# Adding up four of a pair's seven products in one PSUM bank of a Strassen-Winograd matmul

## The chip, the core and the metric

The kernel runs on one core of one Trainium2 chip. The metric is the device time of one execution in microseconds (us). Three runs of the kernel before took 1344.66, 1345.26 and 1346.1 us; their median is 1345.26 us.

## What is computed

One layer of a decoder trunk on x (1 x 1024 x 1024, float32), cut to what matters here:

```python
xn = rmsnorm(x, norm_mix_w)
proj = xn @ w_in                        # 34 blocks of 128 columns
merged = sigmoid(g_da) * (diff_attention(...) @ w_br_da) + sigmoid(g_sw) * (sliding_window(...) @ w_br_sw)
x = x + merged @ w_mix_out
u = rmsnorm(x, norm_ffn_w) @ w_up       # 44 blocks: 22 gate, 22 value
c = causal_conv3(u) + conv_b
x = x + (silu(c_gate) * c_val) @ w_down
return rmsnorm(x, norm_final_w)
```

## The kernel before

All activations are held transposed: channels on the 128 partitions, the 1024 tokens along the free axis. Each float32 operand is split into a high part (a cast to fp32r by ScalarE, tag `wh`, `sh`) and a low part (the rest, by a VectorE subtraction, tag `wl`, `sl`), and each product of blocks is three matmuls: high x high, high x low, low x high.

The stages follow each other on TensorE: `project` (w_in), `attention`, `rest` and `mix` (the branches and w_mix_out), `hidden` (w_up, the convolution, the gating), `down` (w_down). In `project`, `hidden` and the middle of `down`, output blocks are computed in pairs with Strassen's algorithm in Winograd's form: a pair is a 2 x 2 product of blocks, and seven products of 128 x 512 x 512 do the work of eight. Each product (`product`, L879) is 12 matmuls of 128x512. The operands of the weights' side are A11, A12, A22 and the sums S1 to S4, which GpSimd makes (`sum_pair`, L97 to L100); `split_pair` (L111 cast, L113 subtraction) splits them. The tokens' side has B11, B21, B22 and T1 to T4, made once per stage. The products are P1 = A11 B11, P2 = A12 B21, P3 = S4 B22, P4 = A22 T4, P5 = S1 T1, P6 = S2 T2, P7 = S3 T3.

In `project` (loop at L424, nine pairs) and `hidden` (loop at L903, 22 pairs) every product has a PSUM bank of its own, out of eight. `recombine` (L440) then copies P1 out on ScalarE (L446) and does seven VectorE additions (L447 to L453), of which three read a bank and an intermediate result, and all end in the pair's two output tiles `us` (c11 and c12 the halves of the first, c21 and c22 of the second). TensorE goes on with the next pair's products meanwhile.

After that, in `project`, GpSimd multiplies each `us` by the reciprocal norm (L436), and `keep` splits it (ScalarE L465 or L468, VectorE L466 or L469) and stores it for the attention. In `hidden`, GpSimd (L1020) multiplies by the reciprocal norm, and `conv` works out the convolution: one ScalarE activation (L1029) and two VectorE instructions (L1031, L1032) for each of the two tiles; then silu (L1012), a product (L1013) and a store.

What sets the order: each engine issues its instructions strictly in the order in which a scheduler put them when the program was built. Buffers turn over in pools: `wh` and `wl` have two buffers for each shape, so the cast of the weights A11 and A12 of the pair after next takes the buffer that this pair's P1 and P2 read; `sh` and `sl` have three in `hidden`, two in `project` and `down`. A hand-written order exists as well: `issue_after(self.front)` (L1026) puts the convolution of a pair behind the cast and the subtraction of the A11 and A12 loaded last, on ScalarE and on VectorE.

In `down` (loop at L1116, four pairs), the block P1 = A11 B11 stays in a bank `y`, S2 T2 and S3 T3 are added to it there, S1 T1, S4 B22 and A22 T4 have banks of their own, and VectorE adds each to the columns of `x3` that it belongs to.

Of the kernel before, what the change touches and what calls it, by code (L numbers as in the profile page):

```python
# [13 lines left out]
ALU = mybir.AluOpType  # L14
# [3 lines left out]
P = 128  # L18
D = 1024
T = 1024  # L20
KC = D // P
NB = T // P
H2 = 512
DFF = 2816
NF = DFF // P
# [17 lines left out]
class Trunk:  # L43
# [210 lines left out]
    def project(self):  # L254


        nc, tc = self.nc, self.tc
# [3 lines left out]
        with ExitStack() as ctx:  # L261
            e = ctx.enter_context
# [9 lines left out]
            bank = lambda: self.tl(psA, [P, H2], "t")  # L272
            ps = [[bank() for _ in range(2)] for _ in range(3)]
# [10 lines left out]
            def diffs(k):  # L284

                (a, a2), (b, b2) = ([xr[r][:, hf * H2:(hf + 1) * H2] for hf in range(2)] for r in (k, k + 4))
                tt = nc.vector.tensor_tensor
                tt(a, a2, a, ALU.subtract)
                tt(a2, b2, a2, ALU.subtract)
                tt(b2, b2, a, ALU.subtract)  # L290
                tt(b, b2, b, ALU.subtract)

            def parts(k):
                for n, r in enumerate((k, k + 4)):
# [4 lines left out]
            for pool, h, l in ((self.wp, "wh", "wl"), (self.wp, "wh", "wl"), (self.uw, "sh", "sl")):  # L299
                w = self.tl(self.wp, [P, KC, P], "raw", bufs=RAW), self.tl(pool, [P, KC, P], h, F32R), self.tl(pool, [P, KC, P], l, F32R)  # L300
# [12 lines left out]
            with tc.tile_pool(name="xrp", bufs=6, reuse_waits="tile") as xrp:  # L313
# [97 lines left out]
            tp = e(tc.tile_pool(name="tpa", bufs=1, reuse_waits="tile"))  # L411
            for m in self.plain[3:]:
# [4 lines left out]
                if m == self.plain[3]:  # L417
                    with tc.issue_after(self.pow.ins), tc.high_priority(40):
                        wg, pg = self.next_w(), [bank() for _ in range(2)]
                    for hf in range(2):  # L420
                        self.mm3(pg[hf], wg, self.xact, hf)
            prods = (("P1", "A11", "B11"), ("P2", "A12", "B21"), ("P5", "S1", "T1"), ("P7", "S3", "T3"), ("P3", "S4", "B22"),
                     ("P6", "S2", "T2"), ("P4", "A22", "T4"))
            for j, ms in enumerate(self.pairs):  # L424
                w = self.next_w()
                pp = {}
                for name, a, b in (prods[i] for i in ((0, 1, 4, 2, 3, 5, 6) if j == 0 else (0, 1, 2, 5, 3, 4, 6))):
                    pp[name] = bank()
                    self.product(pp[name], w[a], b)
                us = [self.tl(tp, [P, T], "us", bufs=3) for _ in range(2)]  # L430
                self.recombine(pp, us, tp, 0)
                for m, u in zip(ms, us):
                    if self.kind[m] == "g":
                        nc.sync.dma_start(self.gd[m - 18], u)
                    else:
                        nc.gpsimd.tensor_tensor(u, u, self.rstd, ALU.mult)  # L436
                        self.keep(m, u, (tp, "hi"))
        self.uw = None

    def recombine(self, ps, us, tp, o):  # L440
# [3 lines left out]
        s1, u2, u3, u4 = (self.tl(tp, [P, H2], n, bufs=1) for n in ("s1", "u2", "u3", "u4"))  # L444
        tt = nc.vector.tensor_tensor
        nc.scalar.copy(s1, ps["P1"])  # L446
        tt(c11, ps["P2"], s1, ALU.add)  # L447
        tt(u2, ps["P6"], s1, ALU.add)
        tt(u3, ps["P7"], u2, ALU.add)
        tt(c22, ps["P5"], u3, ALU.add)  # L450
        tt(u4, ps["P5"], u2, ALU.add)
        tt(c12, ps["P3"], u4, ALU.add)  # L452
        tt(c21, u3, ps["P4"], ALU.subtract)  # L453

    def keep(self, m, u, to):

# [397 lines left out]
    def operands(self, xt, xtp, xw, k):  # L854

        tt = self.nc.vector.tensor_tensor
        (b11, b12), (b21, b22) = ([xw[kc][:, hf * H2:(hf + 1) * H2] for hf in range(2)] for kc in (k, k + 4))

        def put(name, t):
            hi, lo = self.split(xt[name, k, "h"], xt[name, k, "l"], t)  # L860
            if name == "T13":
                self.B["T1", k], self.B["T3", k] = ((hi[:, c], lo[:, c]) for c in (slice(0, H2), slice(H2, T)))
            else:
                self.B[name, k] = hi, lo

# [11 lines left out]
        tt(t4, t2, b21, ALU.subtract)  # L877

    def product(self, ps, a, b, ks=range(4), first=True, last=True, skip=False, low=False):  # L879

# [9 lines left out]
    def hidden(self, pair):  # L890
        nc, tc = self.nc, self.tc
        with ExitStack() as ctx:
            e = ctx.enter_context
# [9 lines left out]
            for j in range(NF):  # L903
                w, ps = ready.pop(j) if j else (w0, {})
# [17 lines left out]
                if j == NF - 1:  # L922

                    with tc.high_priority(50):
# [5 lines left out]
                for name, a, b in (prods[i] for i in ((0, 1, 2, 5, 3, 6, 4) if j == NF - 1 else (0, 1, 2, 5, 3, 4, 6) if j else range(7))):  # L930
                    if name not in ps:
                        ps[name] = self.tl(psF, [P, H2], "t")
                        self.product(ps[name], w[a], b, low=name == "P1")
                us = [self.tl(tp, [P, T + 2], "us", bufs=3) for _ in range(2)]
                if j == NF - 1:
                    self.defer.pop(0)(lo)
                    self.xctx2.close()
# [5 lines left out]
                self.recombine(ps, us, tp, 2)  # L943
                if j < NF - 1:

                    with nullcontext() if j else tc.issue_after(self.pow.ins):
# [45 lines left out]
    def sums_h(self, k):  # L992

        b11, b12, b22, b21 = (self.raw_h(N1 + j, hf) for j, hf in ((k, 0), (k, 1), (k + 4, 1), (k + 4, 0)))
        tt = self.nc.vector.tensor_tensor
        tt(b11, b12, b11, ALU.subtract)
        self.B["T1", k] = self.parts_h(b11)
        tt(b12, b22, b12, ALU.subtract)
        tt(b22, b22, b11, ALU.subtract)
        self.B["T2", k] = self.parts_h(b22)  # L1000
        self.B["T3", k] = self.parts_h(b12)
        tt(b21, b22, b21, ALU.subtract)
        self.B["T4", k] = self.parts_h(b21)

    def glu(self, j, w, us, tp, after):
# [29 lines left out]
    def down(self):  # L1035

        nc, tc = self.nc, self.tc
        with ExitStack() as ctx:
# [233 lines left out]
```

## Time and profile before

| | us |
|---|---|
| median of three runs | 1345.26 |
| span of the profiled execution, first to last instruction | 1343.0 |
| TensorE busy in it | 1326.8 |
| VectorE busy | 1052.5 |
| ScalarE busy | 602.3 |
| GpSimd busy | 488.8 |

The profiled execution's time outside its span is not shown by itself; the median stands 2.3 us above the span, and that is taken for it. By the timeline, `project`'s pairs are multiplied from 66 to 237 us, `hidden`'s from 677 to 1098 us, and `down` follows. In the profile PE is TensorE's matmul, PEld its weight loading, DVE is VectorE, ACT ScalarE, POOL GpSimd and SP the engine that issues most DMAs. A row of the timeline gives start, duration, engine, line, operation, tiles written <- tiles read, and their shape; what stands in square brackets is idle time of the engine before it and what ended it. A matmul row is longer than the distance to the next one, because matmuls overlap.

### The profile page before, as it was taken

To read this page: it belongs to the slowest core of one execution; us is meant where nothing else is said; L and a number is where in the kernel's file an instruction comes from. 1 tells how busy PE (TensorE), PEld (TensorE's weight loads), DVE (VectorE), ACT (ScalarE), POOL (GpSimd) and SP (SyncE) were. 2 spreads that over 40 slices of the span, in tenths; PEclk is the share of its full clock that TensorE was granted. 3 is DMA by queue.
4 is the path that set the end of the run, shared out by engine and by line. 5 is a ranking of instruction groups with operands and counts; after the bars stand their busy time and mean duration, and the time that the engine had idled before them with its cause. 6 is when DMAs were issued, how large, how long until landed. Compare 5 with 4: busy or idle time off the path is not lost.

```text
span 1343.0 us, 17167 instructions
## 1 busy us (share of the span) xinstructions
PE 1326.8 (99%) x6304; PEld 1105.7 (82%) x6304; DVE 1052.5 (78%) x1425; ACT 602.3 (45%) x929; POOL 488.8 (36%) x364
## 2 busy tenths in 40 slices
PE   8999999999999999999999999999999999999997
PEld 6888888888888878888888888888888888788886
DVE  7846775388898976445669999999999998967454
ACT  8432232276667774344444434343434345432433
POOL 0346652000101016642446566666666611131011
PEclk9999999999999999999999999999999999999998
DMA  7244443966554245324522222222222239642342
GB/s 258 108 146 162 148 149 119 273 170 189 143 148 144 70 155 206 141 95 130 167 79 95 79 79 85 88 79 79 88 85 80 86 128 320 220 145 98 94 141 79
DMA packets 63812, 179.49 MB, mean 134 GB/s; under 512 B 7024, under 2 KB 16880, under 8 KB 63728
## 3 DMA queue, kind: packets, MB, share of 16 engines
q1 hardware_dynamic: 52272, 161.22, 36.8%
q10 hardware_dynamic: 11456, 17.18, 3.5%
q8 instruction: 50, 0.82, 0.2%
q14 instruction: 34, 0.28, 0.1%
HBM read 129.61 MB, written 48.76 MB: 133 GB/s over the span
## 4 chain that ended last, share of the span: by engine, by line
PE 72%; DVE 15%; issue 8%; DMA 2%; ACT 1%; POOL 1%; SPq 0%; POOLq 0%; DVEq 0%; ACTq 0%
PE t L887 24%; PE g L153 4%; PE g L154 4%; PE g L155 4%; DVE c L1031 3%; PE y L1056 3%; PE d L1056 3%; PE sc L154 3%; PE sc L155 3%; PE sc L153 3%; PE d L887 3%; PE sc L619 3%; PE y L887 2%; DVE wl L113 2%; DMA hr<-hd 2%
## 5 line engine op out<-in xcount | busy, mean ns | idle before, releaser
L1020 POOL TENSOR_TENSOR us<-us,rstd 128x1024 f32<-128x1024 f32 x42 | 92.6, 2225 | 85.0 <-DVE us L452 47.6
L1029 ACT ACTIVATE c<-us,vecs 128x1024 f32<-128x1024 f32 x44 | 54.8, 1248 | 118.3 <-POOL us L1020 113.8
L132 ACT CAST wh<-raw 128x1024 fp32r<-128x1024 f32 (+2 forms) x58 | 58.7, 1012 | 107.9 <-PE sc L154 35.8
L134 DVE TENSOR_TENSOR wl<-raw,wh 128x1024 fp32r<-128x1024 f32 (+2 forms) x58 | 78.3, 1352 | 32.5 <-ACT wh L132 22.8
L113 DVE TENSOR_TENSOR sl<-sf,sh 128x1024 fp32r<-128x1024 f32 x62 | 89.3, 1442 | 12.8 <-ACT sh L111 12.8
L111 ACT CAST sh<-sf 128x1024 fp32r<-128x1024 f32 x62 | 64.5, 1042 | 61.6 <-PE t L887 44.0
L97 POOL TENSOR_TENSOR sf<-rv 128x512 f32<-128x512 f32 x30 | 51.3, 1711 | 93.6 <-DVE sl L113 51.1
L1031 DVE SCALAR_TENSOR_TENSOR c<-us,vecs,c 128x1024 f32<-128x1024 f32 x44 | 75.4, 1746 | 2.7 <-ACT c L1029 2.7
L99 POOL TENSOR_TENSOR sf<-raw,rv 128x512 f32<-128x512 f32 x30 | 56.7, 1891 | 46.3 <-DVE sl L113 46.3
L1032 DVE SCALAR_TENSOR_TENSOR c<-us,vecs,c 128x1024 f32<-128x1024 f32 x44 | 73.2, 1696 | 0.0
L153 PE MATMUL g<-xh,wh 128*128 128x512 f32 x176 | 71.0, 403 | 1.5 <-ACT g L548 1.5
L154 PE MATMUL g<-xl,wh 128*128 128x512 f32 x176 | 70.3, 400 | 0.0
L155 PE MATMUL g<-xh,wl 128*128 128x512 f32 x176 | 70.3, 399 | 0.0
L170 POOL TENSOR_TENSOR rs<-ms,mhalf 128x8 f32<-128x8 f32 (+2 forms) x9 | 13.5, 1499 | 155.5 <-DVE ms L168 149.4
L1012 ACT ACTIVATE c<-c 128x1024 f32<-128x1024 f32 x22 | 23.4, 1064 | 89.6 <-DVE c L1032 89.6
L113 DVE TENSOR_TENSOR wl<-raw,wh 128x1024 fp32r<-128x1024 f32 (+1 forms) x35 | 61.8, 1765 | 0.3 <-ACT wh L111 0.2
L602 POOL MEMSET aT<- 128x128 f32 x32 | 6.1, 204 | 151.5 <-PE t L648 101.2
L623 DVE CUSTOM_DVE_ANT_0 L<-sc,bias 128x128 f32<-128x128 f32 (+7 forms) x64 | 47.8, 752 | 16.6 <-PE sc L619 13.7
L98 POOL TENSOR_TENSOR sf<-sf,raw 128x512 f32<-128x512 f32 x31 | 58.2, 1877 | 2.2
L624 ACT ACTIVATE L<-L,sm 128x128 f32<-128x128 f32 (+7 forms) x64 | 49.6, 778 | 20.0 <-DVE sm L623 17.3
L776 POOL TENSOR_TENSOR gr<-gr,rstd 128x1024 f32<-128x1024 f32 x16 | 40.3, 2523 | 43.9 <-DMA gr<-gd 43.7
L113 DVE TENSOR_TENSOR wl<-rv,wh 128x512 fp32r<-128x512 f32 x30 | 54.0, 1800 | 2.6 <-ACT wh L111 2.6
(435 smaller groups left out, 4338.4 us busy)
## 6 DMA issues: line engine op xcount, KB each, us to landing
u<-qd SPq DMA_DIRECT2D x72, 256.0 KB, 6.4
raw<-in_w_down SPq DMA_DIRECT2D x27, 512.0 KB, 3.7
hr<-hd SPq DMA_DIRECT2D x50, 256.0 KB, 4.8
raw<-in_w_up SPq DMA_DIRECT2D x23, 512.0 KB, 3.5
raw<-in_w_in SPq DMA_DIRECT2D x22, 512.0 KB, 3.8
hd<-c SPq DMA_DIRECT2D x22, 512.0 KB, 2.6
rv<-in_w_up SPq DMA_DIRECT2D x21, 512.0 KB, 3.5
gr<-gd SPq DMA_DIRECT2D x16, 512.0 KB, 3.4
```

The costliest lines, as they stand in the source:

```text
L111: cast = nc.scalar.copy(hi, src)
L113: low = nc.vector.tensor_tensor(lo, src, hi.bitcast(F32), ALU.subtract)
L132: self.hi = nc.scalar.copy(wh, raw)
L134: self.lo = (eng or nc.vector).tensor_tensor(wl, raw, wh.bitcast(F32), ALU.subtract)
L153: nc.tensor.matmul(ps, wh[:, kc + o, :], ah, start=first and n == 0, stop=False)
L154: nc.tensor.matmul(ps, wh[:, kc + o, :], al, start=False, stop=False)
L155: nc.tensor.matmul(ps, wl[:, kc + o, :], ah, start=False, stop=last and n == len(kcs) - 1)
L887: nc.tensor.matmul(ps, (ah, ah, al)[p][:, k, :], (bh, bl, bh)[p], start=first and n == p == 0, stop=last and p == 2 and n == len(ks) - 1, ...
L1020: i = (nc.vector if m % NF == 0 else nc.gpsimd).tensor_tensor(us[:, 2:], us[:, 2:], self.rstd, ALU.mult)
L1031: nc.vector.scalar_tensor_tensor(c, us[:, 1:T + 1], cw[1], c, ALU.mult, ALU.add)
L1032: nc.vector.scalar_tensor_tensor(c, us[:, 0:T], cw[0], c, ALU.mult, ALU.add)
L1056: nc.tensor.matmul(ps, v[:, n, :], x, start=n == i == 0, stop=n == len(js) - 1 and i == 2)
```

## The change

Eight of `project`'s nine pairs and 20 of `hidden`'s 22 (all but the first and the last) go through a new function, `chained`, in place of seven products and `recombine`. It uses three banks: y, d and e.

```diff
+        y = bank(); self.product(y, w["A11"], "B11", skip=True, low=low)
+        nc.scalar.copy(c11, y)
+        d = bank(); self.product(d, w["S1"], "T1", skip=True)
+        nc.scalar.copy(c22, d)
+        self.product(y, w["S2"], "T2", first=False, skip=True)
+        nc.scalar.copy(c12, y)
+        e = bank(); self.product(e, w["A12"], "B21")
+        add(c11, e)
+        self.product(y, w["S3"], "T3", first=False, skip=True)
+        add(c22, y)
+        self.product(d, w["S4"], "B22", first=False, skip=True)
+        add(c12, d)
+        self.product(y, w["A22"], "T4", first=False, skip=True)
+        nc.scalar.copy(c21, y)
```

(Shortened: y and e are taken from the banks that hold P1 and P2 where the pair before has started them; `copy` is ScalarE, `add` is one VectorE addition of a bank to the output tile.) The order of the products is P1, P5, P6, P2, P7, P3, P4; before it was P1, P2, P5, P6, P7, P3, P4. A matmul that adds to y must wait until the copy or the addition that reads y's last state is done: P6 waits for c11's copy, P7 for c12's copy, P4 for c22's addition; P3 waits for c22's copy out of d.

`recombine`, which the other pairs keep, copies P1 out twice and does its seven additions in place. T4's sign is turned (L291, L877, L1002), so that A22 T4 is added everywhere. `us` has four buffers in `project` and five in `hidden`, for three.

In `down` the products come in the order S2 T2 (to y), S1 T1 (to a second bank), S3 T3 (to y), S4 B22 (to the second bank), A22 T4 (to y), with one VectorE addition after each, five for seven:

```diff
-                self.product(ps, w["S1"], "T1")
-                for x in (col(m, 1), col(m + 4, 1)):
-                    tt(x, x, ps, ALU.add)
                 self.product(y, w["S2"], "T2", first=False, skip=True)
                 tt(col(m, 1), col(m, 1), y, ALU.add)
-                ps = bank(0)
-                self.product(ps, w["S4"], "B22")
+                self.product(ps, w["S1"], "T1", skip=True)
+                tt(col(m + 4, 1), col(m + 4, 1), ps, ALU.add)
+                self.product(y, w["S3"], "T3", first=False, skip=True)
+                last = tt(col(m + 4, 1), col(m + 4, 1), y, ALU.add)
+                self.product(ps, w["S4"], "B22", first=False, skip=True)
                 tt(col(m, 1), col(m, 1), ps, ALU.add)
-                self.product(y, w["S3"], "T3", first=False, skip=True)
-                for hf in range(2):
-                    last = tt(col(m + 4, hf), col(m + 4, hf), y, ALU.add)
-                ps = bank(0)
-                self.product(ps, w["A22"], "T4")
-                tt(col(m + 4, 0), col(m + 4, 0), ps, ALU.subtract)
+                self.product(y, w["A22"], "T4", first=False, skip=True)
+                tt(col(m + 4, 0), col(m + 4, 0), y, ALU.add)
```

More of the change, by code (lines that the diff above doesn't have):

```diff
@@ L425, in project @@
                 w = self.next_w()
[L426 to L431, printed above, removed]
+                us = [self.tl(tp, [P, T], "us", bufs=4) for _ in range(2)]
+                if j == 0:
+                    pp = {}
+                    for name, a, b in (prods[i] for i in (0, 1, 4, 2, 3, 5, 6)):
+                        pp[name] = bank()
+                        self.product(pp[name], w[a], b)
+                    self.recombine(pp, us, 0)
+                else:
+                    self.chained({}, w, us, bank, 0)
                 for m, u in zip(ms, us):
@@ L438, in project, with recombine, chained @@
         self.uw = None
-    def recombine(self, ps, us, tp, o):
+    def recombine(self, ps, us, o):
         nc = self.nc
         c11, c12, c21, c22 = (us[w][:, o + hf * H2:o + (hf + 1) * H2] for w in range(2) for hf in range(2))
[L444 to L453, printed above, removed]
+        tt = lambda c, a, b: nc.vector.tensor_tensor(c, a, b, ALU.add)
+        for c in (c11, c12):
+            nc.scalar.copy(c, ps["P1"])
+        tt(c11, c11, ps["P2"])
+        tt(c12, c12, ps["P6"])
+        tt(c22, c12, ps["P7"])
+        tt(c21, c22, ps["P4"])
+        tt(c22, c22, ps["P5"])
+        tt(c12, c12, ps["P5"])
+        tt(c12, c12, ps["P3"])
+    def chained(self, ps, w, us, bank, o, low=False):
+        nc = self.nc
+        c11, c12, c21, c22 = (us[w_][:, o + hf * H2:o + (hf + 1) * H2] for w_ in range(2) for hf in range(2))
+        add = lambda c, p: nc.vector.tensor_tensor(c, c, p, ALU.add)
+        y = ps.get("P1")
+        if y is None:
+            y = bank()
+            self.product(y, w["A11"], "B11", skip=True, low=low)
+        nc.scalar.copy(c11, y)
+        d = bank()
+        self.product(d, w["S1"], "T1", skip=True)
+        nc.scalar.copy(c22, d)
+        self.product(y, w["S2"], "T2", first=False, skip=True)
+        nc.scalar.copy(c12, y)
+        e = ps.get("P2")
+        if e is None:
+            e = bank()
+            self.product(e, w["A12"], "B21")
+        add(c11, e)
[5 more added lines that the diff above has]
+        nc.scalar.copy(c21, y)
     def keep(self, m, u, to):
@@ L942, in hidden @@
                         self.ahead(2)
[L943 removed]
+                if split:
+                    self.recombine(ps, us, 2)
                 if j < NF - 1:
```

16 lines of the change are left out of this document (10 added, 6 removed).

## The prediction

> **What bounds the kernel now.** The page's busy times come first, then the stretches of time, then TensorE's waits and its timeline.
>
> ```profile
> span 1343.0 us, 17167 instructions
> PE 1326.8 (99%) x6304; PEld 1105.7 (82%) x6304; DVE 1052.5 (78%) x1425; ACT 602.3 (45%) x929; POOL 488.8 (36%) x364
> ```
> ```profile
> 677.00:1098.00 421.00, 421.00 (x1869) 348.39 (x1868) 410.40 (x356) 171.54 (x189) 246.03 (x170) 1.00 0.24 82
> ```
> ```profile
> PE t L280 <- ACT wh L310: 5.0, 1, 5.0
> ...
> PE d L176 <- POOL rs L170: 1.1, 1, 1.1
> ```
> ```profile
> 849.71 0.39 PE L887 MATMUL t<-T_2h,wl 128*128 128x512 f32 x1
> ...
> 855.83 0.39 PE L887 MATMUL t<-B_3h,wl 128*128 128x512 f32 x1
> ```
>
> TensorE is the bound: idle for 16.2 of 1343.0 us, of which 5.0 are the start. In `hidden` (677 to 1098 us) it never stops. The last fence holds the first and last of 28 matmuls: 6.12 / 27 = 0.227 us from start to start, so 12 matmuls, a product, take 2.72 us and a pair's 84 take 19.04. The change leaves every matmul in place, so in these stages there is nothing to win on TensorE. VectorE is busy 410.40 of the 421.00 us in `hidden`; it keeps up because eight banks stand between the two engines.
>
> **The change part by part.** It removes VectorE additions, four in each of 28 chained pairs and two in each of `down`'s four, and adds three ScalarE copies to each chained pair.
>
> ```profile
> L450 DVE TENSOR_TENSOR us<-t,u x31: 678/692/695, 85.9 to 1101.0; 128x512 f32<-128x512 f32 x31
> L446 ACT COPY s<-t x31: 567/587/591, 69.1 to 1094.4; 128x512 f32<-128x512 f32 x31
> ```
>
> (Durations in ns: least, median, most.) That is 120 x 0.69 = 83 us less on VectorE and 84 x 0.59 = 49 us more on ScalarE. Neither is the bound, so the path gains nothing; a gain could only be what VectorE costs TensorE now, and TensorE's waits name none in `hidden`.
>
> What it adds to the path are the waits inside a pair. TensorE now waits for c11's copy before P6, c12's before P7, c22's addition before P4. I read in the order of the built program what is queued ahead of each reader.
>
> *hidden, P4.* VectorE's order in the chained pairs is: c11's addition, the subtraction `wl` for the A11 and A12 of the pair after next, four convolution instructions, and only then c22's addition, for which P4 waits. The `wl` subtraction waits for its cast on ScalarE, and the cast for P2, the last reader of its buffer. P2 was a pair's second product and is now its fourth, so all of this starts two products later, while P4 is due 5.44 us after P2. TensorE has a little more cover: ten of the next pair's first twelve matmuls stand ahead of P4, so from P2's end it has 34 x 0.227 = 7.71 us of work.
>
> ```profile
> 845.06 0.68 DVE L447 TENSOR_TENSOR us<-t,s 128x512 f32<-128x512 f32 x1
> 845.66 2.42 DVE L113 TENSOR_TENSOR wl<-raw,wh 128x1024 fp32r<-128x1024 f32 x1
> 848.00 3.50 DVE L1031 SCALAR_TENSOR_TENSOR c<-us,vecs,c 128x1024 f32<-128x1024 f32 x2
> 851.43 3.50 DVE L1032 SCALAR_TENSOR_TENSOR c<-us,vecs,c 128x1024 f32<-128x1024 f32 x2
> 854.85 1.21 DVE L113 TENSOR_TENSOR sl<-sf,sh 128x1024 fp32r<-128x1024 f32 x1
> 855.99 1.21 DVE L1013 TENSOR_TENSOR c<-c,c 128x1024 f32<-128x1024 f32 x1
> 857.12 0.68 DVE L448 TENSOR_TENSOR u<-t,s 128x512 f32<-128x512 f32 x1
> ```
> ```profile
> 842.59 4.40 POOL L1020 TENSOR_TENSOR us<-us,rstd 128x1024 f32<-128x1024 f32 x2 [2.08 <-DVE us L452]
> 848.78 1.64 POOL L97 TENSOR_TENSOR sf<-rv 128x512 f32<-128x512 f32 x1 [1.78 <-DMA rv<-in_w_up]
> 850.50 2.15 POOL L98 TENSOR_TENSOR sf<-sf,raw 128x512 f32<-128x512 f32 x1
> ```
> ```profile
> 858.40 1.06 ACT L111 CAST wh<-raw 128x1024 fp32r<-128x1024 f32 x1
> ```
> ```profile
> L1031 DVE SCALAR_TENSOR_TENSOR c<-us,vecs,c x44: 1272/1280/2702, 714.4 to 1142.8; 128x1024 f32<-128x1024 f32 x44
> L113 DVE TENSOR_TENSOR sl<-sf,sh x36: 1209/1215/1711, 719.0 to 1051.3; 128x1024 fp32r<-128x1024 f32 x36
> L99 POOL TENSOR_TENSOR sf<-raw,rv x5: 1291/1297/1302, 125.1 to 201.3; 128x512 f32<-128x512 f32 x5
> ```
>
> Undisturbed, counted from the end of P2's slot: 0.20 until the cast starts (a matmul row lasts 0.39, 0.16 beyond its slot, and a start follows an end by about 0.04); the cast to 1.25; the subtraction, 1.21, to 2.45; four convolution instructions 1.20 apart to 7.25; the addition to 7.93; P4 at 7.99. That is 0.28 us past the 7.71.
>
> It will not be undisturbed. The rows show VectorE and GpSimd taking turns on operands in SBUF: GpSimd's two multiplications end at 846.99 and the `wl` that started at 845.66 ends 1.1 us after that; the convolution instructions take 1.27 alone and about 2.3 with L97 or L98 beside them, which in turn grow from 1.30 to 1.64 and 2.15. The bank-reading additions never exceed 0.695. So each GpSimd instruction between the cast and c22's addition costs about 1.25 us. Which ones are there? One turn, from the start of P4 (0): c times c and c12's addition to 1.7; GpSimd's first multiplication 2.8 to 4.8; P4 done at 2.9, A22's cast to 3.5, its subtraction after GpSimd at 5.4. The load that GpSimd's sums need is issued behind that subtraction; before, the same step took from 845.14 to L97's start at 848.78:
>
> ```profile
> 843.02 2.12 DVE L113 TENSOR_TENSOR wl<-rv,wh 128x512 fp32r<-128x512 f32 x1
> ```
>
> So L97 starts at 9.05. P2's slot ends at 11.33 (P4, two matmuls of P1, then P5, P6, P2). L97 runs to 10.35, VectorE's `sl` to 11.5, L98 to 12.8, where the next `wl` subtraction is waiting; then in turn `wl` 13.95, L99 15.2, a convolution 16.4, L100 17.65, three convolutions 21.25, c22's addition 21.85, P4 at 21.9. A pair lasts 21.9 instead of 19.04 us: **2.9 us** lost, by nearly all of L99 and L100. The first and last chained pairs have other neighbours in the queue and are counted alike. 20 x 2.9 = 58 us. Bounds: 0.3 a pair with GpSimd out of the way (6 us), 5.3 with all four sums in the way (106 us). I take 2.9, as the landing of one load decides, and its 3.64 us is a row.
>
> *project, P6 and P7.* There is no convolution, and c22's addition comes 1.6 us before P4 needs it. But in three transitions (out of the pairs with blocks 2, 12 and 14) ScalarE's order has `keep`'s cast of the last tile ahead of c11's copy, and that cast waits for GpSimd:
>
> ```profile
> 178.64 2.40 POOL L436 TENSOR_TENSOR us<-us,rstd 128x1024 f32<-128x1024 f32 x1 [1.28 <-DVE us L452]
> 182.21 1.30 POOL L99 TENSOR_TENSOR sf<-raw,rv 128x512 f32<-128x512 f32 x1 [1.16 <-DVE sl L113]
> 183.46 2.27 POOL L100 TENSOR_TENSOR sf<-raw,sf 128x512 f32<-128x512 f32 x1
> 185.69 2.85 POOL L436 TENSOR_TENSOR us<-us,rstd 128x1024 f32<-128x1024 f32 x1
> ```
> ```profile
> 181.08 1.16 ACT L465 ACTIVATE hi<-us,vecs 128x1024 fp32r<-128x1024 f32 x1 [2.32 <-POOL us L436]
> ```
>
> From P3's end: c12's addition done at 0.9, the first multiplication to 3.4, `sl` to 4.5, A22's `wl` to 5.05, L99 to 6.35, L100 to 7.65, the second multiplication to 10.05 (the rows took 9.9 us for the four), the cast to 11.25, the copy to 11.85, P6 at 11.9. P6 is due after P4, P1 and P5, at 8.16: 3.7 us, three times. Where the cast stands behind c11's copy it delays c12's (by 0.9 us, twice), and the first chained pair waits about 2 us for `recombine`'s tile in the same way. The sum is 11.1 + 1.8 + 2: **15 us**, between 5 and 20.
>
> *down, and the pairs left alone.* Each addition there is the first or second thing in VectorE's queue when its bank is done, 0.7 us long, with a product of 2.72 in between: 0, within 3 us either way. `recombine` has as many additions as before: 0.
>
> The sum is 58 + 15 = 73 us on 1343.0, a span of 1416; with the 2.3 us by which the median stands above the span, **1418 us**.
>
> One rule has a price of its own. The clock granted is 1.00 in `hidden`, yet the kernel's first seven matmuls, after an idle start, are 0.49 us apart:
>
> ```profile
> 5.00 0.80 PE L280 MATMUL t<-xh,wh 128*128 128x512 f32 x1 [5.00 <-ACT wh L310]
> ...
> 7.94 0.63 PE L280 MATMUL t<-xh,wh 128*128 128x512 f32 x1
> ```
>
> They take 2.94 us where six steps of 0.227 take 1.36: 1.6 us for a restart. The Trainium skill ("TensorE: Matmul & The Clock Gate", Part 1) says that TensorE's clock is halved after an idle window of about 3.4 us; by it the sum stays as it is for waits of 2.9 us, unless a window need not be empty.
>
> **Rivals.** *The waits are hidden* (not slower). If the convolution ended within 7.71 us of P2, no P4 would wait, and VectorE's lighter load could let the stage run at TensorE's pace: 1343 to 1349. For it: undisturbed, only 0.28 us is missing. Against it: GpSimd's L99 cannot start before `sl`, which needs P6's end, so at least one of the four sums falls into the stretch. It decides as soon as the cast no longer waits for P2.
> *Lighter turns*: only one GpSimd instruction falls in, 1.5 us a pair: 30 + 15, 1390.
> *Heavier turns*: a late load puts a third and fourth in, 4.1 us or more a pair: 82 + 15, 1442.
> *The clock falls at each wait*: 20 to 23 restarts of 1.6 us on top: up to 37 us, 1436 to 1455. For it: the waits are long and regular. Against it: nothing in `before` shows a drop after so short a pause.
> *It doesn't do what it says*: the sums in a bank are the same products in another order; I see no such case.
>
> **How the numbers follow.** The forecast of 2.9 us a pair (1400 to 1430): 0.45. Lighter: 0.22. Heavier: 0.13. Clock: 0.12. Hidden: 0.08, of which 0.03 faster, 0.04 the same and 0.01 a little slower. The range from 1375 to 1446 holds the first three and half of the fourth; it leaves out the hidden case and the highest. A measurement of this kernel can tell about 0.2% (2.7 us) from no change; slower by more than that has 0.93.
>
> **What would show it.** In `hidden`, TensorE's waits should name the c22 addition (`add` in `chained`) about 20 times, with some 2.7 us each, its matmuls there should span about 480 us, and VectorE should run four convolution instructions directly before each of these additions. In `project` a few waits of up to 4 us should name c11's copy on ScalarE. `down` should have none. If the waits name ScalarE's copies in `hidden`, or TensorE's row spacing changes from 0.227 with the clock below 1.00, or the waits come mainly from `project`, the working above is wrong; so it is if no wait shows at all.

## The result and the profile after

The kernel after takes 1418.37 us (median of four runs, 1414.12 to 1419.83), the kernel before 1345.08 us beside it: 1.0538 times as long (95% interval 1.0522 to 1.0555). The forecast was 1418. The profiled execution took 1418.64 us, its span is 1416.8.

The page of the kernel after, first the busy times:

```profile
span 1416.8 us, 17031 instructions
PE 1352.0 (95%) x6304; PEld 1115.0 (79%) x6304; DVE 946.3 (67%) x1305; ACT 649.3 (46%) x1016; POOL 488.5 (34%) x364
```

VectorE is 106 us lighter (83 were forecast; the 88 convolution instructions alone took 124 us for 149), ScalarE 47 us heavier, and TensorE, with the same 6304 matmuls, is no longer at 99%. What it waited for (engine, the tile that was to be written, its line, what released it; then us in total, times, longest):

```profile
PE t L917 <- DVE us L462: 28.0, 18, 2.0
PE t L917 <- ACT us L467: 9.6, 4, 3.2
PE t L917 <- ACT us L470: 6.8, 1, 6.8
...
PE t L917 <- ACT us L472: 3.3, 3, 2.9
```

In the new code L917 is the product's matmul, L462 the addition, L467, L470 and L472 the copies of c11, c22 and c12. None of these lines has a counterpart in the kernel before. To see where they fall, I take each stage from its first matmul to the next stage's, in the timeline of each profile (us):

| kernel | projection's pairs | attention to mix | hidden | down | span |
|---|---|---|---|---|---|
| before | 171.4 | 439.0 | 422.0 | 238.1 | 1343.0 |
| after | 190.0 | 444.6 | 472.5 | 236.9 | 1416.8 |
| difference | +18.6 | +5.6 | +50.5 | -1.2 | +73.8 |

(The rest lies ahead of the projection's pairs and behind the last matmul.) So two thirds are in `hidden`, a quarter in `project`, and 5.6 us are in stages whose code is unchanged.

One pair of `hidden` on its three slower engines, VectorE first, then GpSimd, then ScalarE's cast for the weight subtraction, then TensorE around the wait:

```profile
955.02 2.15 DVE L113 TENSOR_TENSOR wl<-raw,wh 128x1024 fp32r<-128x1024 f32 x1 [0.17 <-ACT wh L111]
957.10 3.50 DVE L1066 SCALAR_TENSOR_TENSOR c<-us,vecs,c 128x1024 f32<-128x1024 f32 x2
960.52 2.47 DVE L1067 SCALAR_TENSOR_TENSOR c<-us,vecs,c 128x1024 f32<-128x1024 f32 x2
962.91 0.68 DVE L462 TENSOR_TENSOR us<-us,t 128x512 f32<-128x512 f32 x1
```
```profile
952.68 2.16 POOL L98 TENSOR_TENSOR sf<-sf,raw 128x512 f32<-128x512 f32 x1
954.80 1.29 POOL L99 TENSOR_TENSOR sf<-raw,rv 128x512 f32<-128x512 f32 x1
956.05 2.27 POOL L100 TENSOR_TENSOR sf<-raw,sf 128x512 f32<-128x512 f32 x1
```
```profile
953.93 1.05 ACT L111 CAST wh<-raw 128x1024 fp32r<-128x1024 f32 x1 [1.13 <-PE t L917]
```
```profile
961.44 0.39 PE L917 MATMUL t<-B_1h,wl 128*128 128x512 f32 x1
963.65 0.50 PE L917 MATMUL t<-T_0h,wh 128*128 128x512 f32 x1 [1.82 <-DVE us L462]
```

The chain is the one that the forecast walked through: the cast waits for P2, the subtraction `wl` for the cast, four convolution instructions come next, then c22's addition (962.91), and P4's first matmul starts as it ends. 963.65 - 961.44 is 2.21 us where 0.227 is the pace: the pair loses 2.0 us, and the P4s of undisturbed pairs lie 21.13 to 21.36 us apart, 2.16 more than 19.04 on average. Two GpSimd sums fall beside the chain, L99 beside `wl` (2.15 instead of 1.21) and L100 beside the first convolution instruction (the two took 3.50, where the next two took 2.47).

Some pairs took longer still. This is the view of stretches for four consecutive ones around another wait (length, busy us of PE, PEld, DVE, ACT, POOL, and then the granted clock):

```profile
785.50:789.00 3.50, 3.50 (x17) 2.91 (x16) 3.50 (x4) 1.19 (x2) 1.17 (x1) 1.00 0.54 152
789.00:792.40 3.40, 1.60 (x8) 1.02 (x7) 3.40 (x4) 1.06 (x1) 0.00 (x0) 1.00 0.01 2
792.40:795.80 3.40, 3.40 (x10) 2.66 (x9) 2.41 (x3) 0.00 (x0) 2.05 (x1) 0.50 0.38 154
795.80:799.00 3.20, 3.20 (x16) 2.61 (x15) 0.69 (x1) 1.60 (x3) 2.32 (x3) 1.00 0.03 10
```

After 3.4 us in which TensorE was busy for only 1.60, it runs for 3.4 us at half its clock, and its matmuls are 0.43 us apart:

```profile
792.68 0.63 PE L917 MATMUL t<-T_0h,wl 128*128 128x512 f32 x1
793.11 0.63 PE L917 MATMUL t<-T_1h,wh 128*128 128x512 f32 x1
```

Five such stretches lie in `hidden` behind its first chained pair, and one of 6.8 us lies in that pair.

### The profile page after: what moved, and what is told of

The parts are those of the page before. It is cut to its first block, busy times and chain, and to the rows that moved or that the text cites. A ratio compares the mean times of both kernels' runs of the same rounds, so it can differ in the third digit from the quotient of the medians.

```text
span 1416.8 us, 17031 instructions
## 1 busy us (share of the span) xinstructions
PE 1352.0 (95%) x6304; PEld 1115.0 (79%) x6304; DVE 946.3 (67%) x1305; ACT 649.3 (46%) x1016; POOL 488.5 (34%) x364
## 4 chain that ended last, share of the span: by engine, by line
PE 74%; DVE 13%; POOL 4%; issue 4%; ACT 3%; DMA 1%; SPq 0%; POOLq 0%; ACTq 0%; DVEq 0%
PE t L917 26%; DVE c L1066 4%; PE g L153 4%; PE g L155 4%; PE g L154 4%; PE y L1091 3%; PE d L1091 3%; PE sc L155 3%; PE sc L153 3%; PE sc L154 3%; DVE c L1067 3%; PE y L917 3%; PE sc L649 3%; PE d L917 2%; POOL us L439 2%
## 5 line engine op out<-in xcount | busy, mean ns | idle before, releaser
L113 DVE TENSOR_TENSOR sl<-sf,sh 128x1024 fp32r<-128x1024 f32 x62 | 96.5, 1557 | 124.9 <-ACT sh L111 124.9
L1055 POOL TENSOR_TENSOR us<-us,rstd 128x1024 f32<-128x1024 f32 x42 | 106.3, 2531 | 192.1 <-DVE us L462 137.2
L462 DVE TENSOR_TENSOR us<-us,t 128x512 f32<-128x512 f32 x84 | 57.2, 682 | 39.0 <-PE t L917 31.5
L1066 DVE SCALAR_TENSOR_TENSOR c<-us,vecs,c 128x1024 f32<-128x1024 f32 x44 | 69.1, 1604 | 8.3 <-ACT c L1064 8.2
L97 POOL TENSOR_TENSOR sf<-rv 128x512 f32<-128x512 f32 x30 | 44.9, 1496 | 85.9 <-DVE sl L113 48.7
L100 POOL TENSOR_TENSOR sf<-raw,sf 128x512 f32<-128x512 f32 x31 | 58.2, 1879 | 0.2
L111 ACT CAST wh<-rv 128x512 fp32r<-128x512 f32 x30 | 18.6, 620 | 85.0 <-PE t L917 79.9
L98 POOL TENSOR_TENSOR sf<-sf,raw 128x512 f32<-128x512 f32 x31 | 56.7, 1830 | 2.2
L111 ACT CAST wh<-raw 128x1024 fp32r<-128x1024 f32 (+1 forms) x35 | 35.2, 1005 | 42.6 <-PE t L917 27.5
```

The costliest lines, as they stand in the source:

```text
L100: tt(sb[:, 1], g[:, 1], sa[:, 1], ALU.subtract)
L111: cast = nc.scalar.copy(hi, src)
L113: low = nc.vector.tensor_tensor(lo, src, hi.bitcast(F32), ALU.subtract)
L1055: i = (nc.vector if m % NF == 0 else nc.gpsimd).tensor_tensor(us[:, 2:], us[:, 2:], self.rstd, ALU.mult)
L1066: nc.vector.scalar_tensor_tensor(c, us[:, 1:T + 1], cw[1], c, ALU.mult, ALU.add)
```

## The experiments

Four questions: does each stage pay for its own waits; what makes `hidden`'s wait; what makes `project`'s; and is anything left of the 74 us when both orders are mended? The stages of all twelve kernels, in the same cut as above (us), with the device time and, where it is a median of four or more runs, its ratio to the kernel before (the others ran once):

| kernel | proj. | att. | hidden | down | time | ratio |
|---|---|---|---|---|---|---|
| e1_project | 188.9 | 443.3 | 433.8 | 247.7 | 1388.2 | |
| e2_hidden | 171.4 | 442.1 | 473.3 | 237.0 | 1398.1 | |
| e3_down | 171.4 | 446.2 | 433.8 | 248.1 | 1370.6 | 1.0191 (1.0177 to 1.0205) |
| e8_down_only | 171.4 | 439.2 | 422.0 | 238.6 | 1344.8 | 1.0001 (0.9992 to 1.0010) |
| e4_p2_second | 188.7 | 443.2 | 450.8 | 237.0 | 1393.6 | 1.0363 (1.0349 to 1.0377) |
| e5_half_sums | 188.6 | 443.6 | 431.1 | 236.4 | 1373.5 | |
| e6_filler | 187.4 | 443.6 | 481.3 | 236.2 | 1422.4 | |
| e7_c22_first | 190.0 | 443.1 | 436.5 | 236.5 | 1380.4 | |
| e9_held | 188.7 | 443.3 | 449.4 | 236.4 | 1389.2 | 1.0333 (1.0319 to 1.0347) |
| e10_dve_copies | 176.0 | 445.0 | 473.9 | 236.4 | 1404.8 | |
| e11_ordered | 172.0 | 443.0 | 423.4 | 236.4 | 1349.2 | 1.0038 (1.0025 to 1.0051) |
| e12_hidden_ordered | 171.4 | 439.2 | 423.4 | 236.8 | 1344.3 | 0.9996 (0.9987 to 1.0005) |

### Each part alone

**e1_project**: the hidden layers' pairs go through `recombine` again, and `down` is as before.

```diff
-                split = j in (0, NF - 1)
+                split = True
```

> Only the projection's pairs are chained; the hidden layers' pairs go through recombine with their products in the old order, and down is as before. Theory A (each stage pays for its own waits): the projection keeps its 18.6 us, from the copies of c11 and c12 that stand behind keep's casts on ScalarE, and the hidden layers come back to about 422 us; span 1343 + 19 = 1362, time 1364 (1362 to 1369). Theory B (the loss is the clock, which falls because of waits anywhere): the projection's own half-clock windows (some 10 us of them, 5 us lost) stay and little else, so 1350 to 1355.

`project` kept its loss (188.9), but the time was 24 us above theory A's 1364: `hidden` came back only to 433.8, and `down` was longer (e3 shows why).

**e2_hidden**: `project` and `down` as before, `hidden` chained.

```diff
-                if j == 0:
+                if True:
                     pp = {}
...
+                    self.recombine(pp, us, 0)
```

> Only the hidden layers' pairs are chained; the projection and down are as before. Theory A: 18 waits of about 2.2 us and one of about 7 at c22's addition stay, with the half-clock windows that come with them; hidden stage about 472 us, span 1343 + 51 = 1394, time 1396 (1392 to 1400). If attention's 5.6 us in the kernel after came from a window that the chained hidden layers' first loads or copies cause, it is seen here too and the time is 1401. Rival: the two stages' losses feed each other (a half-clock window in the projection sets where later ones fall), then this and the run with the projection alone don't add up to the whole 73.8 us.

1398.1, two above the forecast; `hidden` took 473.3, as in the kernel after, and `project` 171.4, as before. By the stage times each stage pays for its own waits; the two total times don't add up to the whole, because in e1 the pairs that are not chained go through `recombine` in its new form (e3).

**e3_down**: no pair chained; `down`'s new order, and `recombine` in its new form (two copies, additions in place) for all pairs.

```diff
-                if j == 0:
+                if True:
...
-                split = j in (0, NF - 1)
+                split = True
```

> Only down's new order and recombine's new form (T4's sign turned, so that its additions need no subtraction of it) are kept; projection and hidden layers as before. Down's pairs and pieces were 1.2 us shorter in the kernel after, so 1344 (1343 to 1346). If that was a matter of where the clock's windows fell, no difference: 1345.

Both theories missed: 1370.6, 25 us over the kernel before. TensorE's waits in e3_down name the reason, an addition of `recombine` in its new form:

```profile
PE t L917 <- DVE us L447: 7.7, 15, 0.5
PE d L1118 <- DVE us L447: 7.4, 1, 7.4
```

It is 0.5 us in 15 pairs of `hidden`, which lie some 19.85 us apart for 19.04, and one wait of 7.4 us where `down` begins. Another 7 us are in attention. That form came into e1 and e3 only because I had turned the chained pairs back through it. In the kernel after it serves three pairs, and neither wait shows there. The forecast had put it at 0 because the number of additions stays; that reason does not hold, though the three pairs show no cost.

**e8_down_only**: as e3, with `recombine` in its old form.

```diff
+        tt(c11, ps["P2"], s1, ALU.add)
...
+        tt(c21, u3, ps["P4"], ALU.add)
```

> The kernel before with down's new order alone, and with recombine's old form (one copy, seven additions, T4 with its sign turned) in every other pair. Theory A (the 25 us of the run e3_down are the price of recombine's new form in the hidden layers, 0.8 us a pair and one wait of 7.5 us at the end, and no price of down's order): projection 171.4, hidden 422, down 237 against 238.1, total 1344 (1342 to 1346). Rival (down's order or the turned sign costs something): over 1350. Attention, 443 to 446 us in all seven kernels that copy or add in the new form and 439 before, goes back to 439 if that form's later last loads set it, and stays near 443 if not.

1.0001 (0.9992 to 1.0010): `down`'s new order is worth nothing, and the 1.2 us by which `down` was shorter after are not its doing (238.6 here; e2 has the old order and 237.0). The 25 us of e3 went with the form of `recombine`; the pools of `us`, which e8 brings back to three buffers as well, were not tried apart. And attention went back to 439.2. Its 2316 matmuls, told by the tiles that they write and read, stand in exactly the order of the kernel before here, while in the kernel after and in all others with chained pairs in `project` 772 places of that order hold another matmul, and in e2 and e3 1007: a scheduler laid the unchanged stages out anew around the changed ones.

### What makes hidden's wait

**e4_p2_second**: P1, P2, P6, P5, P7, P3, P4.

```diff
+        e = ps.get("P2")  # ahead of S2 T2
+        add(c11, e)
         self.product(y, w["S2"], "T2", first=False, skip=True)
         nc.scalar.copy(c12, y)
         d = bank()
         self.product(d, w["S1"], "T1", skip=True)
```

> The kernel after with the chained pair's products in the order P1, P2, P6, P5, P7, P3, P4 instead of P2 as the fourth, so that the cast of the weight quarter whose buffer P2 gives back, and with it VectorE's weight subtraction, comes two products (some 7 us) earlier, ahead of the convolution. Theory A (VectorE's order: the addition of c22 is queued behind a weight subtraction that came late, and takes turns with GpSimd's additions): the waits at c22's addition vanish or fall below 0.5 us, the half-clock windows of the hidden layers vanish with them, and P6 in the projection has more cover: 1348 to 1356. Theory C (a pair that adds up in one bank waits whatever the order, because the bank is read on the way and the copies of one pair and the first products of the next collide): waits of about 2 us move to another product, 1395 to 1418. Theory B (the clock would fall in any case at this density of matmuls): waits gone, but half-clock windows stay, 1365 to 1375.

The waits at c22's addition vanished, as theory A had it, but waits of 0.6 to 1.3 us came up elsewhere in 18 pairs, which lie some 20.0 us apart for 19.04, and the time was 38 us above theory A's upper end. TensorE's waits in e4's `hidden`, and ScalarE's timeline in one pair:

```profile
PE t L917 <- ACT us L477: 13.2, 18, 1.3
PE t L917 <- ACT us L474: 4.4, 1, 4.4
PE t L917 <- ACT us L467: 3.0, 1, 3.0
```
```profile
902.82 1.06 ACT L1047 ACTIVATE c<-c 128x1024 f32<-128x1024 f32 x1 [0.95 <-DVE c L1067]
903.78 0.56 ACT L477 COPY us<-t 128x512 f32<-128x512 f32 x1
```

L477 is c22's copy here, for which P3 waits: silu (L1047) stands ahead of it on ScalarE and waits for VectorE's convolution. The queue that was late was exchanged for another. No half-clock stretch lies in these 18 pairs, though each has a wait. `project` did not profit: P6 has one product of cover in this order too.

**e5_half_sums**: GpSimd makes two of the four sums.

```diff
+        if self.half:
+            return g, v, sa, sa
         tt(sb[:, 0], g[:, 0], v[:, 0], ALU.subtract)
         tt(sb[:, 1], g[:, 1], sa[:, 1], ALU.subtract)
```

> The kernel after, but in the hidden layers GpSimd makes only two of the four weight sums of each pair (L97 and L98; the products that would use the other two take these), so this part of the computation is left out and the output is another one. Everything else, the seven products and VectorE's order with the four convolution instructions ahead of c22's addition, stays. Theory A's second half (the stall of 2.2 us at the fourth product P4 comes from VectorE taking turns with GpSimd: without the turns the same queue ends about 0.3 us late): the wait falls from 2.0 us to below 0.5, the half-clock windows of the hidden layers vanish, hidden about 430 us, total about 1376 (1372 to 1384). Rival (the queue order alone makes the stall, turns or not): the wait stays near 2 us, 1410 to 1418.

The order on VectorE is the same, four convolution instructions ahead of c22's addition, but nothing takes turns with them. VectorE's timeline in e5, one pair:

```profile
910.44 1.23 DVE L116 TENSOR_TENSOR wl<-raw,wh 128x1024 fp32r<-128x1024 f32 x1 [0.17 <-ACT wh L114]
911.59 2.48 DVE L1070 SCALAR_TENSOR_TENSOR c<-us,vecs,c 128x1024 f32<-128x1024 f32 x2
913.99 2.47 DVE L1071 SCALAR_TENSOR_TENSOR c<-us,vecs,c 128x1024 f32<-128x1024 f32 x2
916.38 0.68 DVE L465 TENSOR_TENSOR us<-us,t 128x512 f32<-128x512 f32 x1
```

From `wl` to the addition it takes 5.94 us, for 7.89 above. TensorE's waits in e5's `hidden` name that addition once:

```profile
PE t L920 <- ACT us L473: 3.8, 1, 3.8
PE t L920 <- DVE us L465: 0.2, 1, 0.2
```

`hidden` fell from 472.5 to 431.1, the time to 1373.5 (1376 expected). The pairs lie 19.20 us apart, so the queue alone costs 0.16 us a pair. It takes the turns to make the wait, and the queue as well, as e7 will show.

**e6_filler**: six matmuls more ahead of P4, into a bank of their own.

```diff
+        if low:
+            self.product(bank(), w["A22"], "T4", range(2))
         self.product(y, w["A22"], "T4", first=False, skip=True)
```

> The kernel after with six more matmuls in each chained pair of the hidden layers, into a bank that nothing reads, ahead of P4: 6 x 0.227 = 1.36 us of each stall are spent in matmuls instead of waiting. Theory A with the clock as a consequence of the stalls: the wait falls from 2.0 to about 0.7 us, the windows at half clock that come every fourth pair vanish, and the five of them that follow the first one (1.7 us lost each, of which the next pair's shorter stall gives back half) are won: 1410 to 1414. If the windows alone were the price and the stalls cost little besides: 1400. If the stall is set by VectorE's chain and the windows do not depend on the stall's length: 1418, windows as before. If the extra matmuls only push everything that follows: 1418 + 19 x 1.36 = 1444.

1422.4 is none of the four numbers. Six of the next pair's first matmuls moved behind P4 and the filler took their places, so that P4's cover stayed at ten matmuls. Still the wait fell by one us, and its cause is again in the turns. TensorE's waits in e6, then VectorE and GpSimd in one pair:

```profile
PE t L919 <- DVE us L462: 16.5, 18, 1.0
```
```profile
912.77 1.23 DVE L113 TENSOR_TENSOR wl<-raw,wh 128x1024 fp32r<-128x1024 f32 x1 [0.17 <-ACT wh L111]
913.91 3.52 DVE L1068 SCALAR_TENSOR_TENSOR c<-us,vecs,c 128x1024 f32<-128x1024 f32 x2
```
```profile
911.52 1.30 POOL L99 TENSOR_TENSOR sf<-raw,rv 128x512 f32<-128x512 f32 x1 [1.16 <-DVE sl L113]
912.78 2.37 POOL L100 TENSOR_TENSOR sf<-raw,sf 128x512 f32<-128x512 f32 x1
```

In the longer pair L99 is done as `wl` starts, and only L100 takes a turn. P4s lie 21.6 us apart: 19.04 + 1.36 of filler + 1.2. So the loss of a pair is about 0.16 us without a sum in the stretch (e5), 1.2 with one (e6) and 2.16 with two (after): about 1.0 us each. The half-clock stretches behind the first chained pair are gone as well.

**e7_c22_first**: the order of the change, with the preceding pair's convolution written behind c22's addition.

```diff
         add(c22, y)
+        for f in then:
+            f()
```

> The kernel after with the products in its own order (P2 the fourth), but the preceding pair's convolution is written behind c22's addition, so that VectorE has one convolution instruction instead of four between the weight subtraction and that addition. Theory A (queue order on VectorE): the wait at P4 falls from 2.0 us to 0 to 0.7, the half-clock windows vanish with it, hidden 422 to 440 us, total 1368 to 1386. What would speak against it: a wait of the same length at P4, or at P3 or at the next pair's first products because the convolution is late in turn.

The addition now stands behind one convolution instruction instead of four, as VectorE's timeline in one pair shows:

```profile
878.20 2.25 DVE L113 TENSOR_TENSOR wl<-raw,wh 128x1024 fp32r<-128x1024 f32 x1 [0.17 <-ACT wh L111]
880.37 2.30 DVE L1071 SCALAR_TENSOR_TENSOR c<-us,vecs,c 128x1024 f32<-128x1024 f32 x1
882.59 0.67 DVE L462 TENSOR_TENSOR us<-us,t 128x512 f32<-128x512 f32 x1
```

Eight waits of at most 0.9 us at that addition are left, all before 923 us, about the middle of the stage; from 941 us on P4s are 19.04 us apart up to the last chained pair, as the products need it. `hidden` 436.5, time 1380.4, inside theory A's range.

**e9_held**: e4's order and e7's convolution together, and in `project` the preceding pair's `keep` written behind c22's copy.

```diff
         nc.scalar.copy(c22, d)
+        for f in mid:
+            f()
...
         add(c22, y)
+        for f in then:
+            f()
```

> The order P1, P2, P6, P5, P7, P3, P4 of the kernel e4_p2_second, and besides: the preceding pair's convolution is written behind c22's addition (so that SiLU, which waits for the convolution, no longer stands ahead of c22's copy on ScalarE: 1.1 us a pair there), and in the projection the preceding pair's casts are written behind the next pair's copies. Theory A, all waits being matters of queue order: hidden waits below 0.3 us a pair, projection's three waits of 3.2 us below 1, no half-clock window but perhaps one in each stage's first pair, total 1345 to 1358, and not below 1343, since TensorE's 6304 matmuls at their pace set the time of the kernel before as well. Rival (some wait at the shared bank can't be ordered away): 0.5 to 1 us a pair stay, 1365 to 1385.

The rival came nearer (1365 to 1385), and it was too low as well: 1389.2. The wait was moved a second time, back to c22's addition (18 waits of up to 1.1 us). In this order of products nothing of the next pair stands between P3 and P4, and the scheduler issued all four convolution instructions, `sl` and c times c ahead of the addition again, though the convolution is written behind it. VectorE in one pair, with the last two convolution instructions first; P7's last matmul ends at 902.15, and the addition comes 2.7 us later:

```profile
900.14 2.47 DVE L1076 SCALAR_TENSOR_TENSOR c<-us,vecs,c 128x1024 f32<-128x1024 f32 x2
902.54 1.21 DVE L113 TENSOR_TENSOR sl<-sf,sh 128x1024 fp32r<-128x1024 f32 x1
903.67 1.21 DVE L1057 TENSOR_TENSOR c<-c,c 128x1024 f32<-128x1024 f32 x1
904.81 1.27 DVE L464 TENSOR_TENSOR us<-us,t 128x512 f32<-128x512 f32 x2
```

And in `project` the scheduler still put a cast ahead of c11's copy: its three waits of up to 3.1 us stayed. Written order isn't issued order.

### What makes project's wait

**e10_dve_copies**: in `project` VectorE copies c11, c22 and c12.

```diff
-        nc.scalar.copy(c11, y)
+        copy = nc.scalar.copy if low else nc.vector.tensor_copy
+        copy(c11, y)
```

> The kernel after, but in the projection VectorE and not ScalarE makes the copies of c11, c22 and c12; the hidden layers stay. Theory A (the copies are late because they stand behind keep's casts on ScalarE, which wait for GpSimd's multiplication): the three waits of 3.2 us at P6 and the one of 2.9 us at P7 vanish or fall below 1 us, the projection's two to three half-clock windows with them; projection 190.0 to 172 to 178 us, total 1400 to 1407. Rival (VectorE's keep subtraction, which waits for the same cast, takes the copies' place as the thing ahead): waits of 2 to 5 us stay, 1412 to 1425.

This is the kernel after around its first wait for c11's copy in `project`, ScalarE and then TensorE:

```profile
116.50 1.06 ACT L495 ACTIVATE hi<-us 128x1024 fp32r<-128x1024 f32 x1 [5.99 <-POOL us L439]
117.46 0.57 ACT L467 COPY us<-t 128x512 f32<-128x512 f32 x1
```
```profile
118.08 0.50 PE L917 MATMUL t<-t42h,sh 128*128 128x512 f32 x1 [3.05 <-ACT us L467]
```

The copy's bank was ready long before; `keep`'s cast ahead of it had waited for GpSimd's multiplication. With the copies on VectorE, the waits of 3.2 and 2.9 us went (four of at most 0.9 stayed), and `project` fell from 190.0 to 176.0: theory A, 1404.8 of 1400 to 1407.

### Both orders written down

**e11_ordered**: as e7, with the orders made binding for the scheduler.

```diff
+        c12_done = nc.scalar.copy(c12, y)
+        with self.tc.issue_after(c12_done.ins):
+            for f in mid:  # the preceding pair's keep
...
+        c22_done = add(c22, y)
+        with self.tc.issue_after(c22_done.ins):
+            for f in then:  # the preceding pair's convolution
```

> The kernel after in its own order of products, with two orders written down: in the projection the preceding pair's casts are issued behind c12's copy, and in the hidden layers the preceding pair's convolution is issued behind c22's addition. Theory A: projection 171.5 to 176 (waits below 1 us), hidden 422 to 430 (no wait over 0.5 us but in the first chained pair), down 236.5, attention 439 to 444: total 1338 + 0 to 15, so 1340 to 1355, and no faster than before by more than down's 1 to 1.5 us, because TensorE's matmuls at their pace fill the span in both. Rival (ordering one thing back makes the convolution, the stores or c12's addition late in turn): waits of 1 us or more under other names, 1365 to 1385.

1349.2, ratio 1.0038 (1.0025 to 1.0051). `project` 172.0 and `hidden` 423.4; TensorE waits 1.1 us in `hidden` for a copy (0.8 and 0.3) and never in `project`'s pairs. What is left is attention's 4.0 us.

**e12_hidden_ordered**: `hidden` as in e11, `project` as in the kernel before, and with it attention's order of matmuls.

```diff
+                    self.recombine7(pp, us, tp, 0)  # recombine's old form, project only
```

> Chained pairs in the hidden layers only, in the change's own order, with the preceding pair's convolution issued behind c22's addition as in e11_ordered; down in its new order; the projection as in the kernel before (own banks, recombine's old form), by which the scheduler leaves attention's 2317 matmuls in the order that they have in the kernel before. Theory A (attention's 4 us in e11_ordered come from the scheduler's other order of its matmuls, and the chained pairs themselves, once nothing stands in their way, neither cost nor win): attention 439, hidden 422.5 to 424, down 236.5 to 238.5, total 1343 to 1346.5, not to be told from the kernel before. Rival (attention is longer for another reason, such as the memory that the chained pairs take): attention 443, total 1348 to 1350. If lighter VectorE work were worth something at last (it falls by some 70 us): below 1341.

Attention 439.2, time 1344.26 beside 1345.1, ratio 0.9996 (0.9987 to 1.0005). Its busy times:

```profile
span 1342.8 us, 17060 instructions
PE 1326.1 (99%) x6304; PEld 1106.3 (82%) x6304; DVE 967.5 (72%) x1337; ACT 636.0 (47%) x991; POOL 521.1 (39%) x364
```

VectorE works 85 us less than in the kernel before, and the time cannot be told from it. No version here beats the kernel before.

## Why the prediction was right, and where it was not

**The bound** held: nothing was to be won on TensorE, and a lighter VectorE is worth nothing while TensorE runs at 99%. e12 shows it with 1.0 us of waits left in `hidden`.

**hidden, 58 us forecast, 50.5 measured.** The mechanism (cast behind P2, `wl`, four convolution instructions, turns with GpSimd, c22's addition) is shown by e4, e5 and e7, each of which takes away another link, and by e6, in which one of the two turns falls away. TensorE's waits name c22's addition 18 times, where about 20 were forecast, with 0.9 to 2.0 us for 2.7. The mis-sized term is the 2.9 us a pair: it is 2.16. The walk had `wl` waiting as L98 ended, so that the rest of L98 counted besides L99 and L100. In the trace L98 ends at 954.84 and the cast at 954.98: `wl` was not there yet, L99 went first, and two turns of about 1.0 us are left, not 1.25 each and the rest of a third. The Trainium skill ("SBUF — State Buffer", section "SBUF: two separate sides") says that of a VectorE instruction with two inputs in SBUF and a GpSimd instruction that reads SBUF the one that starts first holds the shared ports for its whole length and the other is blocked. The pair shown of the kernel after agrees: `wl` starts at 955.02, 0.22 us behind L99, and takes 2.15 us, that is until L99's end at 956.09 and 1.08 more.

"The first and last chained pairs are counted alike" failed in both directions. The last one does not wait. In the first one, P3 waits 6.8 us for c22's copy, which stands on ScalarE behind pair 0's first convolution step:

```profile
735.12 4.49 DVE L1055 TENSOR_TENSOR us<-us,rstd 128x1024 f32<-128x1024 f32 x2
```
```profile
739.65 1.24 ACT L1064 ACTIVATE c<-us,vecs 128x1024 f32<-128x1024 f32 x1 [0.97 <-DVE us L1055]
740.80 0.57 ACT L470 COPY us<-t 128x512 f32<-128x512 f32 x1
```

The account: 18 x 2.16 = 38.9; the five half-clock stretches 3.6 (the five P4s are 21.84 to 22.02 apart for 21.20, 0.7 each); the first pair the remaining 8.0, with its wait of 6.8 us and a half-clock stretch from 737.8 to 744.6 us.

**project, 15 us forecast, 18.6 measured.** The three waits behind `keep`'s cast are there, 3.1 us on average for the 3.7 forecast, and e10 and e11 show their cause. The first chained pair waited 2.9 for 2, and c12's two waits were 0.2 each for 0.9: together 12.7 us of waits, below the forecast. The rest was missing from the sum: 19 steps from one matmul to the next at half clock, some 0.2 us longer each, are 3.8 us, and 2.1 I cannot assign.

**The clock**, a rival at 0.12, came true in part. The forecast's sum has no term for it, and by the sign that the forecast gave itself (row spacing other than 0.227 with the clock below 1.00) the sum is wrong there: some 7 us in `hidden` and `project` without the first pair of `hidden`. "Nothing in `before` shows a drop after so short a pause" was true and proved nothing, since `before` has no such pauses. In `hidden` it costs less than the rival's 1.6 us at each wait: only each fourth pair or so meets it, and the next wait is shorter in return, so that 0.7 us is left of the 1.4 that seven steps lose (7 x 0.2). The Trainium skill ("TensorE: Matmul & The Clock Gate", Part 1) ties the drop to an idle window of some 3.4 us. Here the window before the drop was not idle but busy for 1.60 of 3.40 us; the rows decide.

**attention, nothing forecast, 5.6 measured.** That a change in one stage can reorder another was not considered at all. e8, e11 and e12 show that about 4 us go with the order of its matmuls; that the order makes them, and not the pool of `us` that changes with it, was not tried. The other 1.6 us separate the kernel after from e11: attention's listed waits are the same in both (3.4 us), but the kernel after has a half-clock stretch from 434.0 to 437.4 us there and e11 has none. At half pace 3.4 us of work lose at most 1.7, so it can be the whole; no run tests it.

**down**: 0 for its own order, as forecast (e8); the 1.2 us less come with `hidden`'s chained pairs (237.0 in e2, with `down` as before).

So 1418 came from a mechanism that was right and from errors that cancel: 7.5 us too much in `hidden`, 1.2 too much in `down`, and 9.2 us too little in `project` and attention together. That the forecast met the time within 0.4 us is luck.

## What to carry to other kernels

A reader that is put into a chain of accumulation must be near the head of its engine's queue when its bank is done. The price of the change was not in its own instructions but in what happened to stand ahead of them. It shrank in `hidden` when their place was written differently (e7), went to other places in the queues under another order of products (e4, e9), and went away when their place was made binding (e11). Fewer instructions on an engine that keeps up were worth nothing here (e12). When a program is rescheduled, compare the order of the stages that were not touched as well.

## What the runs showed of the hardware

In `hidden`, TensorE's clock fell to half for 3.4 us after a 3.4 us stretch in which it was idle for only some 1.8. It fell in about each fourth pair when the listed waits were up to 2.0 us in 21 (after), and in none of the 18 pairs when they were up to 1.3 (e4) or 1.0 (e6).

Where a wait falls decides as well. The five half-clock stretches of the kernel after start at 792.4, 836.8, 922.1, 1007.4 and 1092.8 us, which is 13, 25, 25 and 25 times 3.413 us apart, as windows of that length that run by themselves would have it. The five windows before them were busy for 1.4 to 1.6 us. A wait of 1.87 us, from 876.4 to 878.3, falls into two windows of the same grid, and the clock stayed:

```profile
874.32:877.73 3.41, 2.10 (x10) 1.40 (x8) 3.41 (x4) 1.81 (x2) 0.00 (x0) 1.00 0.12 47
877.73:881.15 3.42, 2.86 (x13) 2.36 (x14) 3.37 (x4) 0.04 (x1) 1.10 (x1) 1.00 0.28 115
```

No sharp limit comes out of these runs: with 1.65 us busy in such a window the clock fell in e2 (940.0 to 943.4) and stayed in e10 (991.1 to 994.5), and in attention it fell after one that was busy for 2.06 (430.6 to 434.0, after).

A sum on GpSimd that falls beside a VectorE instruction with operands in SBUF costs about 1.0 us there (2.15 for 1.21, and 3.50 for 2.47 for a pair of them), and VectorE's 84 additions of L462, which read a bank, keep 0.67 to 0.69 throughout.
